# Feed-forward up projections as seven block products in place of eight, in four parts of a layer

## The chip, the cores and the metric

One Trainium2 chip, one NeuronCore. The metric is device time in microseconds (us) of one execution of the whole program, the median over runs; lower is better. Engines: PE (matrix products, with PEld for its weight loads), DVE (vector), ACT (scalar), POOL (GpSimd), SP (issues the transfers).

## What is computed

Two layers of a hybrid encoder over 512 prompt tokens and 64 sample tokens, 576 columns in all. The feed-forward is the part that the change touches; `D_MODEL` is 1024, `D_FF` is 2816:

```python
x = _layernorm(DEEPNORM_ALPHA * x + merged @ w_o, ln1_g, ln1_b)
ff = (jax.nn.silu(x @ w_ff1) * (x @ w_ff3)) @ w_ff2
x = _layernorm(DEEPNORM_ALPHA * x + ff, ln2_g, ln2_b)
```

Ahead of it every layer has one combined input projection, three attentions (forgetting, differential, sparse), three gated branch products and `w_o`. All inputs and outputs are float32.

## The kernel before

**Numbers in two pieces.** Weights and activations are split into a high piece (a rounded copy, `F32R`) and a low piece (the rest), and each product is three matmuls: high by high, high by low, low by high. A weight tile of 128x512 arrives by a transfer in a staging buffer `st` (three of them); ACT casts it to `wh` (line 331) and DVE subtracts to get `wl` (line 334). The pairs go to a ring of five slots (`RING`, line 42). The tokens lie transposed in `xT`, [128, 8, 1216]: columns 0 to 639 high, from 640 on low.

**Feed-forward.** The 22 blocks of 128 hidden units are done in two parts of 11 (`FF_SPLIT`, line 28). For each block, `s_block` (line 382) makes `x @ w_ff1` and then `x @ w_ff3`: two PSUM banks for the column halves 256 and 320, eight steps over the 1024 inputs, three matmuls and two halves a step, 48 matmuls (line 397). `ff_pair` (line 1624) follows: tanh on ACT (line 1632), two DVE operations from PSUM (lines 1633 and 1643), and the split of the 576-column result into `gT` (ACT line 1650, DVE line 1651). The first block is done by `s_first` (line 406, matmul line 418), half by half, since half 1 holds tokens that come out of the layer norm earlier. After 11 blocks `t_group` (line 356) makes the down projection, `w_ff2`: for two column halves c of 512, five token tiles by 11 blocks, three matmuls each (two for the sample tile; lines 347 to 353), the last blocks tile by tile (`tail`). `adds` (line 1658) adds each tile to `r` on DVE; in the last part c = 1 goes wholly tile by tile (`tail=nf`, line 1784), in the order 4, 3, 2, 0, 1, and each tile goes through `layernorm` (lines 514 to 543: statistics, a power on POOL, three DVE operations of 128x512, one on ACT, one addition on POOL) and, but in the last layer, through `to_xt` (transposes line 441, ACT line 446, DVE line 447) into the next layer's `xT`.

**Order.** Nothing is scheduled by the compiler. The planner `Pace` (line 96) replays the program as it is written, with a cost for each operation, a time from engine to engine (`LAG`) and priorities, and writes each engine's instructions in the order that comes out; on the chip each engine works through its list in that order, waiting for semaphores. `either` lets the planner choose between two engines, `late` makes one of them less welcome.

Of the kernel before, what the change touches and what calls it, by code (L numbers as in the profile page):

```python
# [18 lines left out]
D = 1024  # L19
# [7 lines left out]
NFB = DFF // 128  # L27
FF_SPLIT = (11, 11)
ALPHA = (2 * DEPTH) ** 0.25
# [213 lines left out]
def hybrid_step(ctx, tc, A, O):  # L243
# [56 lines left out]

    def loader(units):
        for u in units:
            st, was = yield take(stage)
            go(fetch(u, st, was))

    def fetch(u, st, was):
        n = 1
# [11 lines left out]
        came = yield dma(128 * n * 4, load, was, 1.5 if u.no == 0 else 4 if u.no < 4 else 5)  # L319
        if u.dest is None:  # L320
            u.slot, free = yield take(ring, u.no)
            hi, lo = u.slot
        else:
            free = yield wait(u.dest[0])
            hi, lo = u.dest[1]()

        def urgent():
            gap = u.no - Unit.used
            return 2 if gap <= 1 else 6 if gap == 2 else 12
# [7 lines left out]
        stage.give(st, down)  # L337
        u.hi, u.lo = view(hi), view(lo)
        u.flag.set(join(up, down))


# [43 lines left out]
    def s_block(units, nk, hi, lo, done, after={}):  # L385
# [16 lines left out]
        for s in range(2):  # L402
            go(done(s, ps[s][0], last))

    def s_first(blocks, X):
# [166 lines left out]

    def give_when(slots, item, flag, kind=None):
        slots.give(item, (yield wait(flag)), kind)

# [62 lines left out]
    def operands(E):  # L638
# [35 lines left out]
        s = yield dve(24, lambda: nc.vector.tensor_scalar(E.gbias, ps[:, :24], 0.5, None, op0=OP.mult), s, 12)  # L674
        banks.give(ps, s, "att")
        E.gbias_in.set(s)

# [770 lines left out]
    def new_env(l):  # L1448
# [4 lines left out]
        one = ("opened", "nt_read", "early_free", "cum", "b_open", "res0_open", "res1_open", "ffn_open",  # L1453
               "mt_open", "gbias_in", "ops", "th_in", "a_prepared")
        for nm in one:
# [7 lines left out]
        E.gb1_in, E.gb2_in = Flag(pace, 2), Flag(pace, 2)  # L1463
        E.ln1 = Flag(pace, 10)
        E.ya, E.yb, E.yc = Flag(pace, 5), Flag(pace, 5), Flag(pace, 5)
        E.close = None
        return E

    def layer_units(E):
# [40 lines left out]
        for part, nf in enumerate(FF_SPLIT):  # L1510
            for f in range(f0, f0 + nf):
                W.f1.append(sblk(w1, D, f * 128))
                W.f3.append(sblk(w3, D, f * 128))
            last = part == len(FF_SPLIT) - 1
            W.f2.append([tcols(w2, 0, f0 * 128, nf),
                         tcols(w2, 512, f0 * 128, nf, (lambda k: None) if not last else (
                             lambda k: None if k == nf - 1 else
                             (E.ffn_open, lambda: (E.res2[:, k, 0], E.res2[:, k, 1]))))])
            f0 += nf
        return W  # L1520


    def in_order(x):
        if isinstance(x, Unit):
# [86 lines left out]
    def open_ffn(E):  # L1611
# [7 lines left out]
        E.gT = fpool.tile([128, max(FF_SPLIT), XW], F32R, name="gT")  # L1619
        E.res2 = fpool.tile([128, FF_SPLIT[-1] - 1, 2, 512], F32R, name="res2")  # L1620
        E.ffn_open.set()
        yield from load_gb(E.gb2, A["ln2_g"][E.l], A["ln2_b"][E.l], E.gb2_in)

    def ff_pair(E, th, part, i):
        tanh = [Flag(pace), Flag(pace)]
        both = Flag(pace, 2)

        def one(h, ps, s):
            c, w = HALVES[h]
            t1, was = yield from th.get()  # L1630
            t = t1[:, c:c + w]
            u = yield act(w, lambda: nc.scalar.activation(t, ps[:, :w], AF.Tanh, scale=0.5), [s, was], 3, 90)  # L1632
            u = yield dve(w, lambda: nc.vector.scalar_tensor_tensor(t, t, 1.0, ps[:, :w], op0=OP.add, op1=OP.mult),  # L1633
                          [s, u], 3)
            banks.give(ps, u, "acc")
            tanh[h].set(u)

        def three(h, ps, s):
            c, w = HALVES[h]
            s = join(s, (yield wait(tanh[h])))  # L1640
# [32 lines left out]
    def layer(E, X, r_free):  # L1673
# [68 lines left out]


        go(open_ffn(E))
        done = [first, second]
        f = 0
        for part, nf in enumerate(FF_SPLIT):
            for i in range(nf):
                th = Later(th_slots)
                one, three = ff_pair(E, th, part, i)  # L1750
                if f == 0:
                    yield from s_first([(W.f1[f], one), (W.f3[f], three)], X)
                else:
                    yield from s_block(W.f1[f], 8, xT, xT_lo, one)
                    yield from s_block(W.f3[f], 8, xT, xT_lo, three)
                f += 1
            before, done = done, [flags5(), flags5()]
            final = part == len(FF_SPLIT) - 1
            if not final:
                for c in range(2):  # L1760
                    yield from t_group(W.f2[part][c], E.gT, adds(E, r, c, True, before[c], done[c]),
                                       ready=E.gT_in[part])
                continue
# [88 lines left out]
```

## Time and profile before

| | us |
|---|---|
| median of 3 runs | 2296.77 (2293.96 to 2298.13) |
| profiled execution, its own time | 2294.76 |
| span of its instructions | 2292.9 |
| PE busy in the span | 2243.2 (98%) |
| DVE, ACT, POOL busy | 1362.6, 979.0, 186.4 |
| granted TensorE clock, share of full | 0.997 |

The span is from the first instruction to the last; the execution's own time has 1.9 us more. "Busy" is the time in which an engine has at least one instruction under way. Matmuls overlap each other, so the duration of one (some 0.3 us) is longer than the distance from one start to the next.

### The profile page before, as it was taken

To read this page: it belongs to the slowest core of one execution; us is meant where nothing else is said; L and a number is where in the kernel's file an instruction comes from. 1 tells how busy PE (TensorE), PEld (TensorE's weight loads), DVE (VectorE), ACT (ScalarE), POOL (GpSimd) and SP (SyncE) were. 2 spreads that over 40 slices of the span, in tenths; PEclk is the share of its full clock that TensorE was granted. 3 is DMA by queue.
4 is the path that set the end of the run, shared out by engine and by line. 5 is a ranking of instruction groups with operands and counts; after the bars stand their busy time and mean duration, and the time that the engine had idled before them with its cause. 6 is when DMAs were issued, how large, how long until landed. Compare 5 with 4: busy or idle time off the path is not lost. (4 is left out here: it accounts for less than half of the span.)

```text
span 2292.9 us, 37910 instructions
## 1 busy us (share of the span) xinstructions
PE 2243.2 (98%) x14564; PEld 2011.9 (88%) x14572; DVE 1362.6 (59%) x2978; ACT 979.0 (43%) x2159; POOL 186.4 (8%) x146
## 2 busy tenths in 40 slices
PE   8999999999999999999999989999999999999998
PEld 7886798789998998999878868987899989989996
DVE  6979664675448443343789896537744474424436
ACT  4565664474333322232345656645743332222221
POOL 1001000201111000000120010002011110000001
PEclk9999999999999999999999999999999999999999
DMA  5321222242342332222332222222323422222222
GB/s 143 99 90 58 72 76 91 85 123 56 102 139 72 91 86 84 84 83 83 106 102 89 92 65 68 77 90 85 118 61 102 147 69 84 83 83 83 85 91 74
DMA packets 248829, 204.79 MB, mean 89 GB/s; under 512 B 24248, under 2 KB 196680, under 8 KB 248648
## 3 DMA queue, kind: packets, MB, share of 16 engines
q1 hardware_dynamic: 248648, 202.37, 29.9%
q8 instruction: 114, 1.87, 0.3%
q14 instruction: 67, 0.55, 0.1%
HBM read 178.26 MB, written 23.92 MB: 88 GB/s over the span
## 5 line engine op out<-in xcount | busy, mean ns | idle before, releaser
L397 PE MATMUL bank<-xT,wh 128*128 128x256 f32 x4416 | 767.5, 296 | 0.0
L397 PEld LDWEIGHTS bank<-xT,wh 128*128 128x128 f32 x4416 | 657.6, 188 | 4.2 <-issue 1.8
L334 DVE TENSOR_TENSOR wl<-st,wh 128x512 fp32r<-128x512 f32 x568 | 400.1, 708 | 409.2 <-ACT wh L331 404.7
L331 ACT CAST wh<-st 128x512 fp32r<-128x512 f32 x568 | 348.6, 620 | 619.6 <-PE bank L397 232.0
L397 PE MATMUL bank<-xT,wl 128*128 128x256 f32 (+1 forms) x2208 | 470.9, 294 | 0.0
L397 PEld LDWEIGHTS bank<-xT,wl 128*128 128x128 f32 x2208 | 368.4, 188 | 0.0
L347 PE MATMUL bank<-wh,xT 128*128 128x512 f32 x560 | 231.8, 414 | 0.0
L349 PE MATMUL bank<-wh,xT 128*128 128x512 f32 x560 | 220.7, 394 | 0.0
L348 PE MATMUL bank<-wl,xT 128*128 128x512 f32 x560 | 220.3, 393 | 0.0
L349 PEld LDWEIGHTS bank<-wh,xT 128*128 128x128 f32 x560 | 105.6, 189 | 23.7
L347 PEld LDWEIGHTS bank<-wh,xT 128*128 128x128 f32 x560 | 105.9, 189 | 19.5 <-ACT c L684 0.9
L348 PEld LDWEIGHTS bank<-wl,xT 128*128 128x128 f32 x560 | 106.1, 189 | 17.6
L347 PE MATMUL bank<-wh,gT 128*128 128x512 f32 x272 | 106.1, 390 | 0.0
L349 PE MATMUL bank<-wh,gT 128*128 128x512 f32 x272 | 105.9, 389 | 0.0
L348 PE MATMUL bank<-wl,gT 128*128 128x512 f32 x272 | 105.9, 389 | 0.0
L976 ACT ACTIVATE P<-bank,nm 128x128 f32<-128x128 f32 (+4 forms) x160 | 80.0, 503 | 59.5 <-DVE nm L985 55.0
L1633 DVE SCALAR_TENSOR_TENSOR th<-th,bank 128x256 f32<-128x256 f32 (+1 forms) x88 | 36.2, 451 | 98.6 <-ACT th L1632 98.6
L985 DVE TENSOR_REDUCE nm<-bank 128x1 f32<-128x384 f32 (+5 forms) x108 | 64.1, 603 | 46.2 <-PE bank L1187 24.2
L764 POOL TENSOR_TENSOR rb<-rb,rc 128x512 f32<-128x512 f32 (+1 forms) x32 | 44.8, 1399 | 563.6 <-DVE rb L759 549.3
L397 PE MATMUL bank<-yhl,wh 128*128 128x256 f32 (+1 forms) x512 | 89.4, 296 | 0.0
L1009 ACT COPY PT<-bank 128x512 f32<-128x512 f32 (+5 forms) x162 | 65.8, 449 | 50.4 <-PE bank L1000 48.3
L1643 DVE SCALAR_TENSOR_TENSOR th<-th,bank 128x256 f32<-128x256 f32 (+1 forms) x88 | 36.2, 451 | 83.1 <-PE bank L397 79.3
(250 smaller groups left out, 3694.1 us busy)
## 6 DMA issues: line engine op xcount, KB each, us to landing
st<-in_w_ff SPq DMA_DIRECT2D x264, 256.0 KB, 2.9
st<-in_w_in SPq DMA_DIRECT2D x256, 256.0 KB, 2.8
st<-in_w_o SPq DMA_DIRECT2D x32, 256.0 KB, 2.9
out<-c SPq DMA_DIRECT2D x18, 256.0 KB, 2.2
m_park<-th SPq DMA_DIRECT2D x16, 288.0 KB, 2.1
merged<-m_park SPq DMA_DIRECT2D x16, 288.0 KB, 5.1
out<-abt SPq DMA_DIRECT2D x16, 256.0 KB, 2.6
st<-in_w_br_a SPq DMA_DIRECT2D x16, 256.0 KB
```

The lines of the kernel that those rows point to most:

```text
L331: up = yield act(n, lambda: nc.scalar.copy(hi[:, :n], st[:, :n]), [came, free], urgent)
L334: return lambda: eng.tensor_tensor(lo[:, :n], st[:, :n], hi[:, :n].bitcast(F32), op=OP.subtract)
L347: nc.tensor.matmul(ps, lhsT=h, rhs=u.hi, start=first, stop=False)
L348: nc.tensor.matmul(ps, lhsT=h, rhs=u.lo, start=False, stop=False)
L349: nc.tensor.matmul(ps, lhsT=lo, rhs=u.hi, start=False, stop=last)
L397: nc.tensor.matmul(ps[s][0][:, :w], lhsT=x[:, kk], rhs=y[:, k, c:c + w], start=(k == 0 and i == 0), stop=(k == nk - 1 and i == 2))
L764: return lambda: eng.tensor_tensor(x[:n], x[:n], buf[:n], op=OP.add)
L976: s = yield act(nk, lambda: nc.scalar.activation(P[:n, j * nk:(j + 1) * nk], S[:n, j * nk:(j + 1) * nk], AF.Exp, bias=nm[:n, j:j + 1], sca ...
L985: return dve(hb * nk, lambda: nc.vector.tensor_reduce(st[0][:n, :hb], S[:n, :hb * nk].rearrange("p (a b) -> p a b", a=hb), axis=AX.X, op=O ...
L1009: ends.append((yield either(act(w, lambda: nc.scalar.copy(PTs[:kw, sl, :n], PT[:kw, sl, :n]), s, 8), late(dve(w, lambda: nc.vector.tensor_ ...
L1633: u = yield dve(w, lambda: nc.vector.scalar_tensor_tensor(t, t, 1.0, ps[:, :w], op0=OP.add, op1=OP.mult), [s, u], 3)
L1643: s = yield dve(w, lambda: nc.vector.scalar_tensor_tensor(t, t, 0.5, ps[:, :w], op0=OP.mult, op1=OP.mult), s, 3)
```

## The change

The weight of two neighbouring blocks of hidden units (1024 inputs by 256 units) is taken as a 2 by 2 matrix of blocks [512 x 128], and the tokens as a 2 by 2 matrix of blocks [512 inputs x 288 columns]. In place of the eight block products a `Group` makes seven, from sums of weight blocks and sums of token blocks, and joins them in PSUM: `seven` makes each as 12 matmuls of 288 columns, lets ACT copy a bank into another one where two results share a part (`start_copy`), and lets DVE add the second product from an SBUF buffer (`added`). 20 of the 22 blocks of a layer go this way (10 groups for `w_ff1`, 10 for `w_ff3`); the first two stay as they were (`PLAIN`). Four sums of weight blocks are made in a group, two on DVE and two on POOL, and seven pieces are split in place of four tiles. The sums of tokens are made once in a layer (`token_sums`). Since the sums and eight `raw` buffers need SBUF, `gT` becomes shorter: the feed-forward is done in parts of 6, 6, 6 and 4 blocks. A matmul of 288 columns opens each bank once in a layer (`seeded`).

```diff
-FF_SPLIT = (11, 11)
+FF_SPLIT = (6, 6, 6, 4)
+PLAIN = 2
+HT = NTOK // 2
+RAW = 8
+EXTRA = 2
...
+        def prepare(self):
+            E, p, came = self.E, self.pieces, self.came
+            if self.before is not None:
+                yield wait(self.before.seated)
+            a11, a21, a22 = self.raw[:3]
+            t = self.sum
...
+            def seat(i, tile, s, made):
+                u = p[i]
+                u.slots = E.more if i in (2, 5) else ring
+                u.slot, free = yield take(u.slots, u.no)
...
+            made = [Flag(pace) for _ in range(7)]
+            in11 = yield wait(came[0])
+            yield from seat(0, a11, in11, made[0])
+            in21 = yield wait(came[1])
+            in22 = yield wait(came[2])
+            s1 = yield comb(t, a21, a22, OP.add, [in21, in22, self.was_sum], "D")
+            yield from seat(1, t, s1, made[1])
+            s3 = yield comb(a21, a11, a21, OP.subtract, [in11, s1], "G")
+            d1 = yield wait(made[1])
+            s2 = yield comb(t, t, a11, OP.subtract, [s1, d1], "D")
+            yield from seat(2, t, s2, made[2])
+            in12 = yield wait(came[3])
+            a12 = self.raw[3]
+            yield from seat(3, a12, in12, made[3])
+            yield from seat(4, a21, s3, made[4])
+            d3 = yield wait(made[3])
+            s4 = yield comb(a12, a12, t, OP.subtract, [d3, s2], "G")
+            yield from seat(5, a12, s4, made[5])
+            yield from seat(6, a22, in22, made[6])
+            self.seated.set()
...
+    def seven(group, E, done):
+        x = join((yield wait(E.sums_in)), (yield wait(E.tmp_free)))
...
+            def emit():
+                for kk in range(4):
+                    for j, (w, part) in enumerate(((u.hi, 0), (u.hi, 1), (u.lo, 0))):
+                        nc.tensor.matmul(bank[:, :HT], lhsT=w[:, kk], rhs=y(kk, part), start=begin and kk == 0 and j == 0,
+                                         stop=kk == 3 and j == 2, skip_group_check=True)
+            s = yield pe(cols(HT, 12), emit, [ok, x, s])
...
+        def start_copy(to, frm, s, flag):
+            flag.set((yield act(HT, lambda: nc.scalar.copy(to[:, :HT], frm[:, :HT]), s, 2, 60)))
...
+        def added(h, bank, s, out):
+            s = join(s, (yield wait(side.flag)))
+            e = side.got
+            s = yield dve(HT, lambda: nc.vector.tensor_tensor(bank[:, :HT], bank[:, :HT], e, op=OP.add), s, 2)
+            side.read.set(s)
+            go(out(h, bank, s))
...
+        a, was = yield bank_acc()
+        p1 = yield from product(0, a, raw(0, 0), True, was)
+        b, was = yield from seeded()
+        go(start_copy(b, a, [p1, was], c[0]))
+        e, was = yield bank_acc()
+        go(aside(e, (yield from product(1, e, made(0), True, was))))
+        u = yield from product(2, b, made(1), False, (yield wait(c[0])))
+        g, was = yield from seeded()
+        go(start_copy(g, b, [u, was], c[1]))
+        c11 = yield from product(3, a, raw(4, 0), False, (yield wait(c[0])))
+        go(done[0](0, a, c11))
+        u7 = yield from product(4, b, made(2), False, (yield wait(c[1])))
+        d, was = yield from seeded()
+        go(start_copy(d, b, [u7, was], c[2]))
+        c12 = yield from product(5, g, raw(4, HT), False, (yield wait(c[1])))
+        go(added(1, g, c12, done[0]))
+        go(added(1, b, join(u7, (yield wait(c[2]))), done[1]))
+        c21 = yield from product(6, d, made(3), False, (yield wait(c[2])))
+        go(done[1](0, d, c21))
+
+    def token_sums(E, X):
+        s = yield from all_of(X.made)
+        yield wait(E.ffn_open)
...
+        for k0 in (0, 2):
...
+                at[r, c] = yield either(dve(2 * HT, whole(nc.vector), [s, used], 5),
+                                        late(gps(2 * HT, whole(nc.gpsimd), [s, used], 5), 0))
...
+            t1 = yield minus(x11, x12, x11, [at[0, 0], at[0, 1]])
+            t3 = yield minus(x12, x22, x12, [at[1, 1], t1])
+            t2 = yield minus(x22, x22, x11, [t1, t3])
+            d1 = yield from parts(0, x11, t1)
+            t4 = yield minus(x21, x21, x22, [t2, at[1, 0]])
+            d2 = yield from parts(1, x22, t2)
+            d3 = yield from parts(2, x12, t3)
+            d4 = yield from parts(3, x21, t4)
+            used = join(d1, d2, d3, d4, t4)
+        E.tmp_free.set(used)
...
         go(open_ffn(E))
+        go(token_sums(E, X))
...
+                two = [ff_pair(E, Later(th_slots), part, i + j, ((0, HT), (HT, HT))) for j in range(2)]
+                for m, g in enumerate((W.f1[f], W.f3[f])):
+                    yield from seven(g, E, [fns[m] for fns in two])
+                i, f = i + 2, f + 2
```

### What moves in the engines' lists

DVE, layer 0, from the end of the first layer norm on (`th` is the work of the first plain blocks, `xT` the last token tile's low piece). Before:

```order
L447 TENSOR_TENSOR xT<-bank_70,xT 128x4x128
L1643 SCALAR_TENSOR_TENSOR th_113<-th_113,bank_69 128x320
L1633 SCALAR_TENSOR_TENSOR th_113<-th_113,bank_74 128x256
L1643 SCALAR_TENSOR_TENSOR th_113<-th_113,bank_73 128x256
L334 TENSOR_TENSOR wl_77<-st_88,wh_76 128x512
L334 TENSOR_TENSOR wl_81<-st_87,wh_80 128x512
L1651 TENSOR_TENSOR gT<-th_113,gT 128x576
```

Now:

```order
L652 TENSOR_TENSOR xT<-bank_70,xT 128x4x128
L1866 SCALAR_TENSOR_TENSOR th_113<-th_113,bank_69 128x320
L586 TENSOR_TENSOR tmp<-xT 128x576
L586 TENSOR_TENSOR fifths<-xT 128x576
L591 TENSOR_TENSOR tmp<-tmp 128x576
L591 TENSOR_TENSOR tmp<-fifths,tmp 128x576
L591 TENSOR_TENSOR fifths<-fifths,tmp 128x576
L1856 SCALAR_TENSOR_TENSOR th_113<-th_113,bank_74 128x256
L596 TENSOR_TENSOR sums<-tmp,sums 128x576
L591 TENSOR_TENSOR tmp<-tmp,fifths 128x576
L395 TENSOR_TENSOR raw_6682<-raw_6680,raw_6681 128x512
```

From behind the `xT` row to the last write of `sums` there are 39 operations on DVE: 20 of 128x576 for the token sums (lines 586, 591, 596), two `gT`, eight weight splits, two weight sums and seven of the two plain blocks' own. POOL has four additions of line 586 and two of line 396 in the same stretch. Layer 1 has the same order.

ACT, in the middle of the blocks of a layer. Before:

```order
L331 CAST wh_82<-st_87 128x512
L331 CAST wh_84<-st_86 128x512
L1650 CAST gT<-th_113 128x576
L331 CAST wh_78<-st_88 128x512
L1632 ACTIVATE th_112<-bank_75 128x256
L1632 ACTIVATE th_112<-bank_68 128x320
```

Now (`bank<-bank` is a start copy, `fifths` a product set aside, `raw` a block or sum of weights, `gT` the end of the pair before):

```order
L352 CAST wh_78<-raw_6680 128x512
L1873 CAST gT<-th_113 128x576
L1873 CAST gT<-th_112 128x576
L532 COPY bank_71<-bank_74 128x288
L352 CAST wh_76<-raw_6679 128x512
L1796 CAST gT<-gT 128x64 x2
L536 COPY fifths<-bank_69 128x288
L352 CAST wh_80<-raw_6683 128x512
L532 COPY bank_72<-bank_71 128x288
```

Before, ACT's list in the blocks had casts, tanh and `gT` alone, and PE waited for none of them but through a weight tile or a bank; now PE's third product of a group stands behind the first copy of this piece.

DVE, the last layer norm (line 707 adds a tile of the down projection to `r`, line 747 is the last addition of a tile). Before:

```order
L542 TENSOR_TENSOR r<-r,gb_16586 128x512
L502 TENSOR_TENSOR r<-r,bank_71 128x512
L514 BN_STATS st_107<-r 128x6
L519 BN_AGGR mv_111<-st_107 128x2
L520 TENSOR_SCALAR mv_111<-mv_111 128x1
L522 SCALAR_TENSOR_TENSOR mv_111<-mv_111 128x1
```

Now:

```order
L747 TENSOR_TENSOR r<-r,gb_16745 128x512
L724 BN_AGGR mv_111<-st_107 128x2
L707 TENSOR_TENSOR r<-r,bank_72 128x512
L725 TENSOR_SCALAR mv_111<-mv_111 128x1
L707 TENSOR_TENSOR r<-r,bank_74 128x512
L719 BN_STATS st_105<-r 128x6
```

Before, a tile's chain stood behind the tile before it, undivided; now the next tiles' additions stand inside it, since a tile is four blocks of matmuls and not eleven.

## Rows read from the trace of the kernel before

**Rows 1.** Page, parts 1: the span, and busy time, share, instructions of two engines.

```profile
span 2292.9 us, 37910 instructions
...
PE 2243.2 (98%) x14564; PEld 2011.9 (88%) x14572; DVE 1362.6 (59%) x2978; ACT 979.0 (43%) x2159; POOL 186.4 (8%) x146
```

**Rows 2.** Windows: the two feed-forward stages, busy time of each engine (instructions), clock, DMA.

```profile
740.00:1109.00 369.00, 369.00 (x2473) 351.09 (x2472) 151.25 (x272) 106.36 (x194) 0.00 (x0) 1.00 0.31 90
1877.00:2245.00 368.00, 368.00 (x2474) 350.44 (x2473) 149.58 (x269) 105.72 (x192) 0.00 (x0) 1.00 0.30 89
```

**Rows 3.** Chain of waits, layer 1: start us, us, what; unbroken runs of up-projection matmuls.

```profile
1877.82 126.39 PE bank L397 x960
...
2074.06 139.04 PE bank L397 x1056
```

**Rows 4.** Groups by form on PE: busy us, mean ns of one, idle before.

```profile
L397 PE MATMUL bank<-xT,wh 128*128 128x320 f32 x2208 | 631.5, 309 | 0.0
L397 PE MATMUL bank<-xT,wh 128*128 128x256 f32 x2208 | 605.9, 283 | 0.0
```

**Rows 5.** Timeline, layer 0, first norm and first block: start us, us, engine, line.

```profile
699.32 0.68 DVE L499 SCALAR_TENSOR_TENSOR r<-r,bank 64x512 f32<-64x512 f32 x1
...
732.70 1.29 DVE L447 TENSOR_TENSOR xT<-bank,xT 128x512 fp32r<-128x512 f32 x2 [1.32 <-ACT xT L446]
...
734.05 0.38 PE L418 MATMUL bank<-xT,wh 128*128 128x256 f32 x1 [0.45 <-DVE xT L447]
...
739.50 0.68 PE L397 MATMUL bank<-xT,wh 128*128 128x256 f32 x4
```

**Rows 6.** Timeline, DVE in the first blocks: two operations back to back in one row.

```profile
740.24 1.29 DVE L334 TENSOR_TENSOR wl<-st,wh 128x512 fp32r<-128x512 f32 x2
...
746.59 0.81 DVE L1633 SCALAR_TENSOR_TENSOR th<-th,bank 128x256 f32<-128x256 f32 x2
```

**Rows 7.** Timeline, POOL and DVE at 61 us.

```profile
61.15 1.29 POOL L764 TENSOR_TENSOR rb<-rb,rc 64x512 f32<-64x512 f32 x1 [1.65 <-DVE rb L759]
...
61.39 1.61 DVE L334 TENSOR_TENSOR wl<-st,wh 128x512 fp32r<-128x512 f32 x1 [0.41 <-ACT wh L331]
```

**Rows 8.** Groups by form on DVE and POOL: busy us, mean ns, idle before.

```profile
L541 DVE TENSOR_TENSOR r<-r,gb 128x512 f32<-128x512 f32 x32 | 20.7, 688 | 0.5
...
L542 DVE TENSOR_TENSOR r<-r,gb 128x512 f32<-128x512 f32 x16 | 25.1, 1570 | 0.4
...
L764 POOL TENSOR_TENSOR rb<-rb,rc 128x512 f32<-128x512 f32 x26 | 36.3, 1396 | 537.3 <-DVE rb L759 527.0 <-ACT P L1052 5.2 <-ACT c L684 5.1
...
L543 POOL TENSOR_TENSOR r<-r,gb 128x512 f32<-128x512 f32 x16 | 26.3, 1641 | 28.3 <-DVE r L541 28.3
```

**Rows 9.** Timeline, PE, end of layer 0: its last column half begins; layer 1's half 0.

```profile
1109.73 0.39 PE L352 MATMUL bank<-res,gT 128*128 128x512 f32 x1
...
1159.93 0.38 PE L418 MATMUL bank<-xT,wh 128*128 128x256 f32 x1 [0.34 <-DVE xT L447]
```

**Rows 10.** Chain of waits, the end of the program.

```profile
2269.81 0.23 PE bank L349
...
2282.73 0.24 PE bank L349
...
2287.61 1.63 DVE r L542
```

**Rows 11.** Windows in layer 1's attentions and a wait there: columns as in rows 2.

```profile
1317.00:1323.10 6.10, 2.96 (x16) 1.99 (x16) 5.91 (x12) 4.16 (x8) 1.53 (x2) 1.00 0.22 86
1323.20:1326.50 3.30, 3.30 (x9) 2.53 (x9) 3.20 (x6) 0.79 (x2) 0.00 (x0) 0.50 0.50 159
...
1322.97 0.67 PE L352 MATMUL bank<-wh,xT 128*128 128x512 f32 x1 [1.86 <-DVE rb L735]
```

**Rows 12.** Groups by form on ACT: busy us, mean ns, idle before.

```profile
L331 ACT CAST wh<-st 128x512 fp32r<-128x512 f32 x568 | 348.6, 620 | 619.6 <-PE bank L397 232.0 <-PE bank L352 207.7 <-issue 112.1
...
L1009 ACT COPY PT<-bank 128x256 f32<-128x256 f32 x28 | 10.3, 374 | 5.3 <-PE bank L1000 4.8 <-ACT Qd L957 0.4
```

More of the change, by code (lines that the diff above doesn't have):

```diff
@@ L301, in loader, with fetch @@
     def loader(units):
+        group = None
         for u in units:
+            if isinstance(u, Group):
+                yield wait(u.E.ffn_open)
+                u.before, group = group, u
+                for j in range(4):
+                    u.raw[j], u.was[j] = yield take(u.E.raws)
+                    go(u.load(j))
+                    if j == 2:
+                        u.sum, u.was_sum = yield take(u.E.raws)
+                        go(u.prepare())
+                continue
             st, was = yield take(stage)
-            go(fetch(u, st, was))
-    def fetch(u, st, was):
+            go(fetch(u, st, was, group))
+    def fetch(u, st, was, group):
         n = 1
@@ L320, in fetch @@
         if u.dest is None:
+            if group is not None:
+                yield wait(group.seated)
             u.slot, free = yield take(ring, u.no)
@@ L325, in fetch, with split @@
             hi, lo = u.dest[1]()
+        yield from split(u, st, n, hi, lo, came, free, view)
+        stage.give(st, u.split)
+    def split(u, st, n, hi, lo, came, free, view):
         def urgent():
@@ L403, in s_block, with raw, made, product @@
             go(done(s, ps[s][0], last))
+    def seven(group, E, done):
+        x = join((yield wait(E.sums_in)), (yield wait(E.tmp_free)))
+        def raw(k0, c):
+            return lambda kk, part: xT[:, k0 + kk, part * LX + c:part * LX + c + HT]
+        def made(i):
+            return lambda kk, part: E.sums[:, i, part, kk]
+        def product(i, bank, y, begin, s):
+            u = group.pieces[i]
+            ok = yield wait(u.flag)
+            if begin:
+                E.whole.add(id(bank))
+            def emit():
[4 more added lines that the diff above has]
+            s = yield pe(cols(HT, 12), emit, [ok, x, s])
+            u.free(s)
+            return s
+        def seeded():
+            bank, s = yield bank_acc()
+            if id(bank) not in E.whole:
+                E.whole.add(id(bank))
+                s = yield pe(cols(HT), lambda: nc.tensor.matmul(bank[:, :HT], lhsT=xT[:, 0, :128], rhs=xT[:, 0, :HT],
+                                                                start=True, stop=True), [s, x])
+            return bank, s
+        def start_copy(to, frm, s, flag):
+            flag.set((yield act(HT, lambda: nc.scalar.copy(to[:, :HT], frm[:, :HT]), s, 2, 60)))
+        def aside(e, s):
+            buf, was = yield take(E.fifth, 3)
+            s = yield act(HT, lambda: nc.scalar.copy(buf, e[:, :HT]), [s, was, x], 3, 60)
+            banks.give(e, s, "acc")
+            side.got = buf
+            side.flag.set(s)
+            E.fifth.give(buf, (yield wait(side.read)))
+        def added(h, bank, s, out):
[4 more added lines that the diff above has]
+            go(out(h, bank, s))
+        side = Env()
+        side.flag, side.read = Flag(pace), Flag(pace, 2)
+        c = [Flag(pace) for _ in range(3)]
+        a, was = yield bank_acc()
[17 more added lines that the diff above has]
+        go(done[1](0, d, c21))
@@ L571, in get, with give_when @@
             return self.item, was
[L573 to L574 removed]
+    def give_when(slots, item, flag, kind=None, more=()):
+        slots.give(item, join((yield wait(flag)), *more), kind)
     def all_of(flags):
@@ L1760, in layer @@
                 for c in range(2):
-                    yield from t_group(W.f2[part][c], E.gT, adds(E, r, c, True, before[c], done[c]),
+                    yield from t_group(W.f2[part][c], E.gT, adds(E, r, c, part == 0, before[c], done[c]),
                                        ready=E.gT_in[part])
```

110 lines of the change are left out of this document (91 added, 19 removed).

## Prediction

> **What bounds the kernel now.** I read the busy times first: PE is busy for 2243.2 of 2292.9 us, DVE for 59% and ACT for 43% [rows 1]. That share alone does not say that a matmul less is time less, so I went to the windows of the two feed-forward stages. There PE is busy for 369.00 of 369 and 368.00 of 368 us, with DVE at 150 to 151 (41%), ACT at 106 (29%), POOL at nothing, and the clock at full [rows 2]. The chain of waits says the same in another way: 960 and 1056 up-projection matmuls follow each other without one wait [rows 3]. So the stage that the change works on is purely PE's, and what is taken from PE there counts in full, as long as nothing else takes its place. The reader should look at what has room: DVE has 218 us free in 369, but not everywhere. Around the two layer norms it is DVE that sets the pace: the first norm's five tiles take DVE from 699.32 to 733.99 us, some 7 us a tile, with hardly a pause [rows 5].
>
> **The matmuls (−62.2 us).** 3840 matmuls of 256 and 320 columns go, 3360 of 288 columns and eight opening ones come: 472 fewer. The distance from one start to the next is 126.39 us / 960 = 0.1317 us in a mix of equal numbers of 256 and 320 [rows 3]; 288 is the middle of the two, and the durations of the two forms, 283 and 309 ns, differ by about what 64 columns cost [rows 4], so I take 0.1317 for 288 as well. 472 x 0.1317 = 62.2 us. The Trainium skill, on its page "TensorE: Matmul & The Clock Gate", section Back-to-back issue gap, gives N/2.4 + 2.5 ns for a lone stream; at 288 columns that would be 122.5 ns, and the saving 57.8 us in place of 62.2. The row is slower than the rule by 9 ns a matmul, and the row decides. The down projection keeps its matmuls.
>
> **The start of each feed-forward (+26 us, 11 to 33).** All seven products wait for the token sums, the first one too, though it reads none. The sums can begin when the last piece of `xT` is written, at 733.99 in layer 0 [rows 5]. From there DVE's list has 39 operations to the last sum: 22 of 576 columns, ten of 512, seven of 256 to 320. Back to back a 512-wide one takes 1.29 − 0.69 = 0.60 us [rows 6], a 576-wide one by the same rate 0.675, a pair of the small ones 0.81 [rows 6]. That is 14.9 + 6.0 + 2.8 = 23.7 us. In the same stretch POOL adds six times, and there a price comes in that the change does not show: a subtraction on DVE that began 0.24 us after a POOL addition took 1.61 us in place of 0.69, 0.92 more, and ended 0.56 us after POOL did [rows 7]; additions that always run beside POOL's average 1570 ns, the same form without it 688 [rows 8]. Both read two SBUF operands, as all the sums do. POOL's 512-wide addition takes 1.40 us alone [rows 8], a 576-wide one by that rate 1.57. Four of these, on which the differences wait, cost DVE 6.3 us and the two narrower ones 0.92 each: 8.1. So the sums stand at 23.7 + 8.1 = 31.8 us after `xT`. PE's own work until then is half 0, 739.50 − 734.05 = 5.45 us [rows 5], and 96 matmuls of the second block, 12.6: 18.1 us. PE then waits 13.7; I take 13 a layer, since a POOL addition may lie partly beside an operation that reads PSUM. Below, without any blocking, it is 23.7 − 18.1 = 5.6; above, with POOL at 1.64 us as in its other group [rows 8], 16.3.
>
> **The end of each feed-forward (+20 us, 14 to 23).** In the last column half the tiles now end after 4 blocks and not 11, so seven blocks, 7 x 14 x 0.23 [rows 10] = 22.5 us of PE's work, no longer stand beside the norms. Layer 0: before, 50.2 us pass from the first matmul of that half to layer 1's half 0, which needs all of `xT` [rows 9]; less 22.5 that leaves 27.7. Now DVE sets it: first tile 8 x 0.23 = 1.8, 0.2 to DVE, and the 34.7 us that the same five tiles take it in the first norm [rows 5]: 36.7, so +9. Layer 1: without `xT` (5.6 us) and 0.9 of other work in that stretch it is 28.2, so DVE ends 30.2 after the half began. Before it ended 35.4 (154 matmuls) + 6.3 after it (2287.61 + 1.63 − 2282.97) [rows 10], and 41.7 − 22.5 = 19.2: +11. The tiles' chains now lie inside each other, which can hide up to 3 us of waiting for POOL in each: hence 14.
>
> **The clock (+3.4 us, 0 to 7).** After waits of 1.9 us and one before it, the granted clock stood at 0.50, 1.2 GHz, for 3.30 us, and then at 1.00 again [rows 11]. PE has no wait of that length in the feed-forward now; ahead of the first group it would stand for some 10 us. I count one such stretch a layer, 3.3 / 2 = 1.7 us of work lost.
>
> **Inside the groups (+4 us, 0 to 32).** For two blocks PE now has 14 x 12 x 0.1317 = 22.1 us. DVE has 18 operations of 512, 12 of 288 and two of 576: 10.8 + 4.8 + 1.4 = 17.0 us, and four POOL additions that cost it up to 0.92 each: 20.7, or 94%. ACT has 14 casts, ten copies and the tanh and `gT` casts, 31 operations of at most 0.62 [rows 12], below 16 us. Weight pieces have a lead of seven products, 11 us, so their lateness is covered. What is not covered is ACT's list: a start copy has one product, 1.58 us, from the end of the bank that it reads to the product that needs it; itself it takes about 0.40 (0.374 at 256 columns), and a cast that has just begun ahead of it 0.62 [rows 12]. With 0.2 for each way, 0.2 to 0.8 is left. Ahead of it ACT may wait for a sum or a `gT` that DVE makes, so a block of 0.92 on DVE can reach PE with some 0.4. I let one in eight of the 80 additions do so: 4 us. All of them: 32.
>
> The added additions to `r` (40 more on DVE), the seven splits for four, and the transfers (the same megabytes) I cost at nothing: the down projections cover them. From the last pair of a part to the end of the next part's first pair DVE's list has 46 operations of 512 (weight splits, additions to `r`, sums of weights), 12 of 288 and two `gT`, 27.6 + 4.8 + 1.4 = 33.8 us, beside some 60 us of PE (22.1 for the pair, 6 x 28 x 0.23 = 38.6 for the down projection). If that cover went, the groups' DVE share would be over 100%, and the third rival below would be the result.
>
> **The sum.** −62.2 + 26 + 20 + 3.4 + 4 = −8.8 us against the profiled execution's 2294.76: 2286.0. The median of the runs lies 2.0 above that execution, so 2288.0 beside 2296.77. A difference under 0.2%, 4.6 us, is what a measurement of this kernel can hardly tell from none.
>
> **The rivals.**
> - *The starts are hidden* (0.15). DVE and POOL do not stand in each other's way here, and the planner's order gets the sums done 5.6 us late; no stalls in the groups, no clock lost: −62.2 + 11 + 20 = −31, 2266. For it: DVE is only 41% busy [rows 2]. Against it: [rows 7, 8].
> - *Starts and ends at their upper ends* (0.10): 33 + 23 in place of 26 + 20 gives 2298, no difference that can be told.
> - *The groups go at the pace of DVE and ACT* (0.22). POOL's additions make DVE late, ACT waits in its list, and the start copies behind it come too late for PE. At 0.4 us each, the gain of 12.8 that is left without this term is gone from 32 of the 80 additions on; with 65 of them it is 26 us, 2310, slower than before. For it: each mid-part pair asks 94% of DVE, in a fixed order that knows nothing of the blocking. Against it: the lead of seven products, and a down projection after at most three pairs.
>
> **How the numbers follow.** The forecast, the terms as I took them, has 0.53: 2288, and from 2280 to 2299 by the bounds of the two large terms, of which 0.38 lies under 2292 and 0.15 between 2292 and 2301. With the first rival that makes faster 0.53, with the second one same 0.25, and the third is slower, 0.22. The range of eight in ten goes from the first rival to a little past the third: 2264 to 2314; the forecast's own is 2280 to 2299.
>
> **What would show it.** In the new profile: matmuls of 288 columns 0.13 us apart; a wait of some 13 us on PE ahead of the first product of each layer's groups, released by DVE's last subtraction of the sums; DVE operations with two SBUF operands at 1.5 us beside POOL's; PE done some 17 us before the end, not 6; in the groups short waits on ACT's copies that sum up to a few us. I am wrong if PE's wait ahead of the groups is under 6 us, or if the groups themselves take over 23 us a pair.

## The result and the profile after

| | before | after |
|---|---|---|
| median, us | 2296.77 | 2269.69 (2268.16 to 2271.98, 5 runs) |
| ratio to before | | 0.9884, 95% interval 0.9869 to 0.9898 |
| span of the profiled execution | 2292.9 | 2267.4 |
| PE busy | 2243.2 | 2196.1 |
| DVE, ACT, POOL busy | 1362.6, 979.0, 186.4 | 1617.9, 1116.4, 319.7 |

The changed kernel is 27.1 us (1.2%) faster. The forecast was 8.8 us, with a range of 2264 to 2314; the time lies in the range and on the side that was forecast, but outside the forecast's own 2280 to 2299, and nearer the first rival's 2266 than the forecast's 2288.

**Where the time went.** Four marks divide the two executions: the first matmul of column half 0 of the feed-forward's first block in layer 0, the first matmul of half 0 of layer 1's first products, the same as the first mark in layer 1, and the end. The timeline on PE, the marks in the kernel before:

```profile
733.21 0.38 PE L418 MATMUL bank<-xT,wh 128*128 128x256 f32 x1 [0.28 <-ACT xT L446]
1159.20 0.39 PE L418 MATMUL bank<-xT,wh 128*128 128x256 f32 x1 [0.24 <-ACT xT L446]
1871.38 0.38 PE L418 MATMUL bank<-xT,wh 128*128 128x256 f32 x1 [0.28 <-ACT xT L446]
```

and in the changed kernel:

```profile
734.02 0.38 PE L623 MATMUL bank<-xT,wh 128*128 128x256 f32 x1 [0.28 <-ACT xT L651]
1148.45 0.40 PE L623 MATMUL bank<-xT,wh 128*128 128x256 f32 x2
1858.37 0.39 PE L623 MATMUL bank<-xT,wh 128*128 128x256 f32 x1 [0.28 <-ACT xT L651]
```

Layer 0's feed-forward goes from 425.99 to 414.43 us (−11.6), layer 1's, to the end of the span, from 421.5 to 409.0 (−12.5). The stages that the change does not touch differ by +0.8 up to the first mark and −2.3 in layer 1's attentions. In the kernels below these stages differ by as much without an edit there (layer 1's take 708.6 to 713.5 us), so I count it as scatter.

So each feed-forward gains 12 us. The matmuls alone are worth 28.5 us a layer (below); some 16 go back, at two places.

**The groups themselves.** The chain of waits (start us, us, what) has a part of three pairs as one unbroken row, in both layers:

```profile
844.47 67.11 PE bank L516 x504
...
1968.22 67.10 PE bank L516 x504
```

That is 67.11 / 504 = 0.1332 us for a matmul of 288 columns, and not one wait. The windows of this part, its down projection and two further stretches (columns as in [rows 2]):

```profile
762.00:766.60 4.60, 4.60 (x19) 4.60 (x20) 4.52 (x6) 1.15 (x3) 1.66 (x1) 0.50 0.58 168
844.50:911.50 67.00, 67.00 (x505) 66.90 (x504) 59.30 (x94) 39.50 (x88) 15.94 (x11) 1.00 0.31 91
911.70:949.70 38.00, 38.00 (x170) 31.45 (x169) 18.62 (x28) 9.45 (x17) 1.29 (x1) 1.00 0.30 89
1130.00:1146.00 16.00, 11.31 (x56) 10.54 (x57) 15.18 (x27) 5.07 (x9) 8.88 (x10) 0.68 0.31 110
```

In the groups PE is busy for all of 67.00 us, with DVE at 59.30 of 67 (89%); in the down projection DVE falls to half. In layer 0's feed-forward the granted clock is below full in two places: behind the wait at the first group (0.50, that is 1.2 GHz, at 762 us) and in the norm at the end of layer 0 (0.68, where the kernel before has 1.00 from 1109 to 1160 us).

**The first group.** Timeline on PE, layer 0:

```profile
753.13 0.43 PE L516 MATMUL bank<-xT,wh 128*128 128x288 f32 x2
...
755.65 0.29 PE L516 MATMUL bank<-sums,wh 128*128 128x288 f32 x1
757.08 0.40 PE L516 MATMUL bank<-sums,wh 128*128 128x288 f32 x1 [1.14 <-DVE sums L596]
...
757.72 0.29 PE L516 MATMUL bank<-sums,wl 128*128 128x288 f32 x1
761.88 0.61 PE L516 MATMUL bank<-sums,mh 128*128 128x288 f32 x1 [3.86 <-ACT bank L532]
```

The first product starts at 753.13, right behind the plain blocks, while DVE still works on the token sums. The second one stops 1.3 us for the second half of its sum, the third one 4.0 us for a start copy of ACT: 5.3 us of waiting. Up to there DVE has no room (windows, columns as in [rows 2]):

```profile
734.00:753.00 19.00, 18.53 (x144) 18.34 (x145) 18.93 (x26) 8.25 (x16) 6.47 (x4) 1.00 0.49 149
753.00:762.00 9.00, 4.00 (x29) 3.53 (x27) 9.00 (x16) 5.97 (x12) 1.74 (x1) 0.91 0.11 29
```

It is busy for 18.93 of 19.00 and 9.00 of 9.00 us. The third product's first matmuls then go at half rate. In the chain 36 matmuls and an opener take from 761.88 to 769.41, 7.5 us in place of 4.9:

```profile
761.88 3.25 PE bank L516 x12
...
765.36 4.05 PE bank L516 x24
769.55 4.78 PE bank L516 x36
```

Layer 1 waits 5.5 us there and loses 2.0 to the clock.

**POOL beside DVE.** Timeline on DVE in the same stretch: four operations of 0.68 to 0.75 us that take longer beside POOL's additions; and the end of the last sum.

```profile
735.11 1.21 DVE L586 TENSOR_TENSOR tmp<-xT 128x576 f32<-128x576 f32 x1
...
741.75 1.74 DVE L355 TENSOR_TENSOR wl<-st,wh 128x512 fp32r<-128x512 f32 x1
...
746.62 2.00 DVE L596 TENSOR_TENSOR sums<-tmp,sums 128x576 fp32r<-128x576 f32 x1
748.55 1.93 DVE L355 TENSOR_TENSOR wl<-raw,wh 128x512 fp32r<-128x512 f32 x1
...
761.92 0.75 DVE L596 TENSOR_TENSOR sums<-tmp,sums 128x576 fp32r<-128x576 f32 x1
```

With one more of 1.12 us these are 4.4 us of being held up. The groups by form show the same for the whole kernel (busy us, mean ns, idle before): a split beside POOL's weight sums takes 957 ns on average, one elsewhere 719.

```profile
L355 DVE TENSOR_TENSOR wl<-st,wh 128x512 fp32r<-128x512 f32 x422 | 301.1, 719 | 232.6 <-ACT wh L352 228.6 <-PE bank L1178 0.9 <-PE bank L1562 0.7
L355 DVE TENSOR_TENSOR wl<-raw,wh 128x512 fp32r<-128x512 f32 x200 | 189.9, 957 | 17.9 <-ACT wh L352 15.8
```

**The end.** Timeline of PE's last matmul, in the kernel before and in the changed one, and of DVE's last addition in the changed one:

```profile
2282.57 0.39 PE L349 MATMUL bank<-wh,gT 128*128 128x512 f32 x1
```

```profile
2248.49 0.39 PE L440 MATMUL bank<-wh,gT 128*128 128x512 f32 x1
```

```profile
2262.09 1.63 DVE L747 TENSOR_TENSOR r<-r,gb 128x512 f32<-128x512 f32 x1
```

PE's last matmul begins 18.9 us before the end of the span, 10.4 before the change (2282.57 of 2292.92); the chain of that time is almost all DVE's. In layer 0 the last 12 us before the second mark are PE's again: from 1136.57 to 1148.45 us it has no wait, and the chain has 20 matmuls of layer 1's half 1 at half clock,

```profile
1137.32 5.58 PE bank L623 x20
```

0.28 us each in place of 0.147 (the half's later ones, 9 in 1.32 us).

### The profile page after: what moved, and what is told of

The parts are those of the page before. It is cut to its first block, busy times and chain, and to the rows that moved or that the text cites. A ratio compares the mean times of both kernels' runs of the same rounds, so it can differ in the third digit from the quotient of the medians.

```text
span 2267.4 us, 37802 instructions
## 1 busy us (share of the span) xinstructions
PE 2196.1 (97%) x14092; PEld 1964.5 (87%) x14100; DVE 1617.9 (71%) x3308; ACT 1116.4 (49%) x2501; POOL 319.7 (14%) x234
## 4 chain that ended last, share of the span: by engine, by line
PE 81%; DVE 12%; issue 4%; POOL 1%; ACT 1%; DMA 1%; SPq 0%; POOLq 0%; DVEq 0%; ACTq 0%
PE bank L488 20%; PE bank L516 20%; PE bank L438 8%; PE bank L440 8%; PE bank L439 8%; PE bank L1177 2%; PE bank L1367 2%; PE bank L1206 2%; PE bank L443 2%; PE bank L444 2%; PE bank L623 2%; PE bank L1178 2%; DVE wl L355 2%; DVE rc L962 1%; PE bank L1528 1%
## 5 line engine op out<-in xcount | busy, mean ns | idle before, releaser
L488 PE MATMUL bank<-xT,wh 128*128 128x256 f32 x1856 | 326.4, 298 | 0.0
L488 PEld LDWEIGHTS bank<-xT,wh 128*128 128x128 f32 x1856 | 275.6, 188 | 4.1 <-issue 1.8
L355 DVE TENSOR_TENSOR wl<-raw,wh 128x512 fp32r<-128x512 f32 x200 | 189.9, 957 | 17.9 <-ACT wh L352 15.8
L516 PE MATMUL bank<-sums,wh 128*128 128x288 f32 x960 | 195.6, 295 | 2.5 <-DVE sums L596 2.5
L488 PE MATMUL bank<-xT,wl 128*128 128x256 f32 (+1 forms) x928 | 197.9, 295 | 0.0
L352 ACT CAST wh<-raw 128x512 fp32r<-128x512 f32 x200 | 123.1, 619 | 77.0 <-PE bank L443 62.5
L516 PEld LDWEIGHTS bank<-sums,wh 128*128 128x128 f32 x960 | 154.0, 188 | 2.9 <-DVE sums L596 2.9
L488 PEld LDWEIGHTS bank<-xT,wl 128*128 128x128 f32 x928 | 154.9, 188 | 0.0
L516 PE MATMUL bank<-sums,wl 128*128 128x288 f32 x480 | 141.5, 295 | 0.0
L516 PE MATMUL bank<-xT,wh 128*128 128x288 f32 x640 | 131.4, 297 | 0.0
L438 PEld LDWEIGHTS bank<-wh,xT 128*128 128x128 f32 x560 | 106.2, 190 | 19.6 <-ACT c L890 0.9
```

The costliest lines, as they stand in the source:

```text
L352: up = yield act(n, lambda: nc.scalar.copy(hi[:, :n], st[:, :n]), [came, free], urgent)
L438: nc.tensor.matmul(ps, lhsT=h, rhs=u.hi, start=first, stop=False)
L488: nc.tensor.matmul(ps[s][0][:, :w], lhsT=x[:, kk], rhs=y[:, k, c:c + w], start=(k == 0 and i == 0), stop=(k == nk - 1 and i == 2))
L516: nc.tensor.matmul(bank[:, :HT], lhsT=w[:, kk], rhs=y(kk, part), start=begin and kk == 0 and j == 0, stop=kk == 3 and j == 2, skip_group_c ...
```

## Experiments

Ten kernels. All times are medians beside runs of the kernel before on the same chip (2295.99 to 2296.74 us). The changed kernel ran only in the first set; differences to it compare medians of different sets, in which the kernel before lay within 0.8 us of itself. The four marks divide each profiled execution, so that the feed-forwards can be told from the stages that no edit touches. After the result the theory was: the gain of the matmuls is real and full; what is given back lies at the first group of each layer (token sums not ready) and at the end of each layer (last part too short); the groups cost nothing.

**1. The four parts alone**, in the kernel before:

```diff
-FF_SPLIT = (11, 11)
+FF_SPLIT = (6, 6, 6, 4)
```

This kernel multiplies `r` by the norm's factor in each of the three first parts and not in one, so it computes something else than the layer; the operations are as many as in the changed kernel's parts, and either form of them takes some 0.68 us.

> The kernel before with one line changed: the feed-forward in parts of 6, 6, 6 and 4 blocks, no block products. Theory (the end of a layer costs because its last column half has tiles of 4 blocks and not 11, so that the norms stand alone): the matmuls stay, layer 0 loses 9 us at its end and layer 1 8.5, with some 1 us of half clock behind the wait: 2296.8 + 18.5 = 2315 us, and PE done some 19 us before the program ends. Rival (the ends are long because DVE and POOL are crowded by sums of the groups): 2297 us, PE done 10 us before the end.

Measured: 2316.3 us, ratio 1.008 (1.0058 to 1.0102): 19.6 us slower, for 18.5 expected. The feed-forwards take 434.8 and 430.3 us, 8.8 more each; the rest lies in the stages without an edit. Timeline: PE's last matmul begins at 2295.42, the span ends at 2314.4, 19.0 us later.

```profile
2295.42 0.39 PE L349 MATMUL bank<-wh,gT 128*128 128x512 f32 x1
```

The end term belongs to the split into parts and has nothing to do with the block products.

**2. Four plain blocks ahead of the groups**

```diff
-PLAIN = 2
+PLAIN = 4
```

> The changed kernel with four plain blocks ahead of the groups and not two. Theory (PE's wait at the first group, 5.6 us a layer, and the half clock behind it, 2.2, are the token sums not being ready): both go, 15.6 us in two layers; two blocks by eight products in place of seven cost 192 x 0.1317 - 168 x 0.1332 = 2.9 us a layer: 2269.7 - 15.6 + 5.8 = 2260 us. Rival (the wait is one of a first group as such: its copies on ACT, its weights): it stays and moves by two blocks, 2269.7 + 5.8 = 2275 us.

Measured: 2261.98 us (ratio 0.9848, 0.9830 to 0.9865), 7.7 faster than the changed kernel, for 9.7 expected; the feed-forwards alone are 5.2 and 4.5 us shorter, which is the 9.7. In the chain PE goes from the plain blocks into the first groups without a stop, and the first product of a group takes 1.59 us, at full rate:

```profile
741.08 37.92 PE bank L488 x288
779.00 1.59 PE bank L516 x12
```

So the wait is not one of a first group as such. It is that for the token sums and what stands between them in DVE's list; 25 us more of other work on PE hide it, at the price of one pair of blocks without the saving.

**3. Parts of 4, 6, 6 and 6**

```diff
-FF_SPLIT = (6, 6, 6, 4)
+FF_SPLIT = (4, 6, 6, 6)
...
-                             lambda k: None if k == nf - 1 else (E.more_free, lambda: E.taken[k]) if k < EXTRA else
+                             lambda k: None if k > EXTRA else (E.more_free, lambda: E.taken[k]) if k < EXTRA else
...
-        E.res2 = fpool.tile([128, FF_SPLIT[-1] - 1 - EXTRA, 2, 512], F32R, name="res2")
+        E.res2 = fpool.tile([128, 1, 2, 512], F32R, name="res2")
```

> The changed kernel with parts of 4, 6, 6 and 6 blocks; in the last column half three weight tiles wait in the ring of five and not one, as there is no room for more resident ones. Theory (tiles of 4 blocks are too short to cover the norms): two blocks more stand beside them, 2 x 14 x 0.23 = 6.4 us a layer, as long as DVE is behind: 2269.7 - 12.8 = 2257 us, PE done 12.5 us before the end and not 18.9. Rival (DVE's order of the chains is what takes the time, whatever PE does beside it; or the ring with three slots taken holds up the next layer's first weights): 2270 us or more.

Measured: 2261.67 us (0.9846, 0.9829 to 0.9863), 8.0 faster than the changed kernel. The feed-forwards take 409.3 and 404.7 us, 5.2 and 4.3 less, for 6.4 expected; the last matmul begins 14.1 us before the end and not 18.9. Theory, at two thirds to four fifths of its price: what is missing was not separated (DVE's chains of the norms, or the three ring slots that are taken).

**4. The token sums on DVE alone**

```diff
-                at[r, c] = yield either(dve(2 * HT, whole(nc.vector), [s, used], 5),
-                                        late(gps(2 * HT, whole(nc.gpsimd), [s, used], 5), 0))
+                at[r, c] = yield dve(2 * HT, whole(nc.vector), [s, used], 5)
```

> The changed kernel with all first additions of the token sums on DVE, none on POOL. Theory (POOL's additions hold DVE up for about as long as DVE would take for them itself): DVE has 4 x 0.67 = 2.7 us more a layer and loses some 3 us of being held up (operations of 1.21, 2.00 and 1.93 us in place of 0.75, 0.75 and 0.68): within 2 us of 2269.7. Rival (POOL's help is real and the wait at the first group ends with DVE's list): 2 x 2.7 = 5.4 us more, 2275 us.

Measured: 2277.11 us (0.9911, 0.9893 to 0.9928): slower by 7.4, near the rival's time. Of the 8.5 us by which the profiled execution is longer, 1.5 and 2.5 lie in the feed-forwards; 0.9 and 3.6 lie in the stages before them, which the edit does not touch. And what the feed-forwards lose is not lost for the rival's reason. From half 0's first matmul (734.90) to the start of the last token sum (761.37) 26.5 us pass, in the changed kernel 27.9 (734.02 to 761.92): DVE is done earlier without POOL's help. But PE waits 6.75 us for the start copy. The timeline of POOL, ACT and PE says why:

```profile
759.04 4.80 POOL L396 TENSOR_TENSOR raw<-raw,raw 128x512 f32<-128x512 f32 x1 [9.31 <-ACT sums L594]
763.87 0.62 ACT L352 CAST mh<-raw 128x512 fp32r<-128x512 f32 x1 [3.87 <-POOL raw L396]
764.40 0.61 ACT L352 CAST wh<-raw 128x512 fp32r<-128x512 f32 x1
764.92 0.39 ACT L532 COPY bank<-bank 128x288 f32<-128x288 f32 x1
765.36 0.61 PE L516 MATMUL bank<-sums,mh 128*128 128x288 f32 x1 [6.75 <-ACT bank L532]
```

A weight sum on POOL took 4.80 us, where 1.30 is the median of its kind in the changed kernel; a cast of ACT waited 3.87 us for it, and the start copy stands behind that cast in ACT's list. DVE ran operations with two SBUF operands without a pause from 758.23 until 762.72, and POOL's addition ended 1.1 us after that:

```profile
758.83 0.74 DVE L595 TENSOR_TENSOR sums<-fifths,sums 128x576 fp32r<-128x576 f32 x1
...
762.04 0.68 DVE L355 TENSOR_TENSOR wl<-raw,wh 128x512 fp32r<-128x512 f32 x1
764.52 0.69 DVE L355 TENSOR_TENSOR ml<-raw,mh 128x512 fp32r<-128x512 f32 x1 [1.80 <-ACT mh L352]
```

The Trainium skill, on its page "SBUF — State Buffer", section "Who interferes with whom", says that of the two engines the one that issues second is fully blocked, whichever it is. The trace agrees that it goes both ways, 2.00 us for a DVE operation of 0.75 and 4.80 for a POOL addition of 1.30; the POOL addition here stood through six DVE operations, not one.

**5. Each product waits, in the plan, for its own token sum**

```diff
-        x = join((yield wait(E.sums_in)), (yield wait(E.tmp_free)))
...
+            x = (yield wait(E.sums_in[{1: 0, 2: 1, 4: 2, 6: 3}[i]])) if i in (1, 2, 4, 6) else {}
...
```

> The changed kernel, planned with each product waiting only for the token sum that it reads, so that the first start copy stands five rows earlier in ACT's list (ahead of three casts of token sums). Theory (the wait at the first group is DVE's list of work: sums, splits and weight sums): the low piece of the third product's weights and the last part of its token sum keep their places in that list within two rows, so PE's wait ends within 1 us of where it did: 2268 to 2271 us. Rival (PE waits only because the copy stands behind casts in ACT's list): the third product starts 2.4 us earlier in each layer, 2265 us.

Measured: 2270.87 us (0.9883, 0.9869 to 0.9898), no difference. PE's waits in layer 0 become 1.5, 1.9 and 1.6 us, 5.0 in all for 5.3. The third product starts 25.7 us after the first mark and not 27.9, nearly as much earlier as the rival said, but it stops again at 763.57, for 1.13 us, until DVE has written its `sums`. The copy's place in ACT's list alone was not the limit: DVE's list is as long as before.

**6. All weight sums on DVE**

```diff
-            s3 = yield comb(a21, a11, a21, OP.subtract, [in11, s1], "G")
+            s3 = yield comb(a21, a11, a21, OP.subtract, [in11, s1], "D")
...
-            s4 = yield comb(a12, a12, t, OP.subtract, [d3, s2], "G")
+            s4 = yield comb(a12, a12, t, OP.subtract, [d3, s2], "D")
```

> The changed kernel with all four sums of weight blocks of a group on DVE and none on POOL. Theory (the groups have room, and POOL's additions cost DVE about what they take off it): 80 more additions of 0.60 us, 48 us, and the splits beside POOL's additions fall from a mean of 957 ns to about 720, 200 x 0.24 = 48 us: DVE's busy time within 15 us of 1618, no wait of PE in the groups, 2267 to 2273 us. Rival (DVE is close to its limit in the groups): waits of PE in the groups, 2280 us or more.

Measured: 2269.65 us (0.9882, 0.9866 to 0.9899), no difference. DVE has 80 instructions more and is busy for 1602.8 us, 15.1 less than in the changed kernel. Groups by form on DVE:

```profile
L355 DVE TENSOR_TENSOR wl<-raw,wh 128x512 fp32r<-128x512 f32 x200 | 135.7, 684 | 16.8 <-ACT wh L352 16.4
L395 DVE TENSOR_TENSOR raw<-raw,raw 128x512 f32<-128x512 f32 x160 | 109.6, 685 | 8.4 <-DMA raw<-in_w_ff 6.8
```

The splits fall from 957 to 684 ns. POOL's additions took 54.2 us from DVE in these splits alone (189.9 − 135.7), and 6.8 in those of `ml`; the 80 additions more on DVE are 54.6. A POOL addition saves DVE nothing here.

**7. Both: POOL adds nothing at the first group** (the edits of 4 and 6)

> Both moves at once: token sums and weight sums all on DVE, so POOL adds nothing at the first group. Theory from the run with the token sums alone on DVE (PE's wait of 6.9 us ended late because a cast of weights, ahead of the start copy in ACT's list, waited for a POOL addition that took 4.80 us beside a busy DVE): that addition now takes 0.7 us on DVE and the wait is some 2 us shorter in each layer, 2277 - 4.5 = 2272 us. Rival (DVE's list alone sets it): two more operations in it, 2278 us or more.

Measured: 2273.17 us (0.9890, 0.9876 to 0.9905), 3.9 faster than run 4, for 4.5 expected; the feed-forwards are 2.1 and 2.7 us shorter than there. The waits in layer 0 are 1.7, 1.7 and 1.4 us, 4.8 in all, and the row on the start copy is now

```profile
767.06 0.85 PE L516 MATMUL bank<-sums,mh 128*128 128x288 f32 x2 [1.12 <-ACT bank L532]
```

That agrees with the cause found in run 4. The wait is close to the changed kernel's 5.3 with any sharing of the sums but that of run 4: what bounds it is DVE's list. The 3.5 us to the changed kernel do not lie in the feed-forwards, which take 413.9 and 408.8 us for 414.4 and 409.0; the first mark comes 5.9 us later in this execution (739.87 for 734.02), in a stage without an edit.

**8. Four plain blocks and parts of 4, 6, 6 and 6** (the edits of 2 and 3)

> The changed kernel with four plain blocks and parts of 4, 6, 6 and 6. Theory (the wait at the start and the short last part are two costs that do not touch each other): the gains of the two single runs add up, 2269.7 - 7.7 - 8.0 = 2254 us. Rival (one of them hides the other, or the first part without groups moves the wait elsewhere): 2258 us or more.

Measured: 2254.4 us, ratio 0.9815 (0.9800 to 0.9830): 15.3 us faster than the changed kernel and 42 faster than the kernel before, the best version here. The two costs are independent: 7.7 + 8.0 = 15.7, and in the feed-forwards 10.4 and 9.1 us are gained where runs 2 and 3 together gain 10.3 and 8.9.

**9 and 10. How far the groups are from DVE's pace.** Useless additions on DVE in the chain of each group's weight sums, four, then eight:

```diff
+            if self.before is not None and self.before.E is E and self.before.before is not None and self.before.before.E is E:
+                d1 = join(d1, (yield wait(E.tmp_free)), (yield wait(E.gb2_in)))
+                for _ in range(4):
+                    d1 = yield dve(512, lambda: nc.vector.tensor_tensor(E.tmp[:, 0, :512], E.gb2[:, 0, :512], E.gb2[:, 1, :512], op=OP.add), [s1, d1], 5)
```

> The changed kernel with four useless DVE additions of 128x512 (two SBUF operands, into a scratch buffer) in the chain of each group's weight sums, from a layer's third group on: 4.8 us more DVE work a pair of blocks, where DVE is now busy for 59.3 of 67.0 us in three pairs. Theory (the lead of seven products, 11 us, covers a DVE that falls behind by less than that, and the down projection lets it catch up): 14.4 - 7.7 = 6.7 us behind after three pairs, no wait of PE in the groups, 2268 to 2274 us. Rival (the groups go at DVE's pace as soon as it has more work than PE): 6.7 us in each of four parts of three pairs and 4.4 in each of four of two, 2269.7 + 44 = 2314 us.

> The same with eight useless additions a group, 9.6 us a pair. Theory: 28.8 - 7.7 = 21 us behind after three pairs, of which the lead covers 11: PE waits some 10 us in each of the four long parts and 3 in each short one, 2269.7 + 52 = 2322 us, with waits released by splits of weights on DVE late in each part. Rival (all of it shows): 21 and 14 us a part, 2410 us; or none of it, 2270, if DVE's list lets the needed splits pass ahead of the sums.

Measured: 2301.56 us with four (ratio 1.0022, 1.0013 to 1.0032), 2417.97 with eight (1.0526, 1.0509 to 1.0544). The theory falls in both. A part of three pairs with four (window of its groups):

```profile
844.50:917.80 73.30, 69.01 (x507) 67.36 (x506) 68.60 (x114) 39.29 (x87) 21.22 (x11) 1.00 0.28 83
```

and with eight:

```profile
851.60:943.10 91.50, 74.51 (x505) 71.66 (x504) 87.33 (x137) 41.66 (x89) 18.86 (x11) 0.94 0.23 67
```

The part takes 73.3 and 91.5 us for 67.1: 6.2 and 24.4 more, where the expectations put the overload at 6.7 and 21 (by their 0.60 us an addition DVE would have 110% and 132% of PE's 67.0 us to do). About the whole overload shows, with eight somewhat more, in part at a lower clock (0.94); a lead of seven products covers none of it. DVE is busy for 94% and 95% of these windows, so even here not all the time. The additions stand one behind the other in the chain of a group's weight sums, and what they cost as a chain was not separated from what they cost as work. The waits on PE in the whole program (us in total, times, longest), in the changed kernel,

```profile
PE bank L516 <- ACT bank L532: 7.7, 2, 3.9
```

with four,

```profile
PE bank L520 <- ACT bank L536: 22.1, 14, 3.9
```

and with eight:

```profile
PE bank L520 <- ACT mh L352: 53.4, 30, 2.8
PE bank L520 <- DVE ml L355: 45.7, 36, 1.7
```

(Lines 532 and 536 are the start copy, 516 and 520 the product.) The 7.7 us are the first groups. With four additions PE waits for late start copies, with eight for the weight pieces themselves, as was expected, but for much longer. The short parts lose less than the rival's 4.4 (1.2 and 2.2 in layer 0), hence 32 us and not 44 with four.

## Why the prediction came out as it did

The terms, as forecast and as measured on the two profiled executions (span 25.5 us shorter, where 8.8 were forecast):

| term | forecast | measured |
|---|---|---|
| matmuls | −62.2 | −57.1 |
| start of each feed-forward | +26 | +10.8 (5.3 and 5.5) |
| half clock behind it | +3.4 | +4.6 (2.6 and 2.0) |
| end of each feed-forward | +20 | +17.6 (9.1 and 8.5) |
| inside the groups | +4 | 0 |
| other stages | 0 | −1.5 |
| sum | −8.8 | −25.6 |

The end's 9.1 is what is left of layer 0's −11.6 after 28.5 for the matmuls, 5.3 and 2.6; layer 1's 8.5 is the longer tail, 18.9 − 10.4, seen directly. In layer 0 it can be seen directly too: from the first matmul of the last column half to the mark 36.2 us pass (1112.30 to 1148.45), before 49.5 (1109.73 to 1159.20), less 22.5 for the seven blocks: 9.2.

**Matmuls: right, 5 us too much.** "I take 0.1317 for 288 as well": 288 columns cost 0.1332, 1.5 ns more than the middle of 256 and 320, and 3360 x 0.0015 = 5.0. The formula on the Trainium skill's page "TensorE: Matmul & The Clock Gate", section Back-to-back issue gap, led to a saving of 57.8, near the measured 57.1 but by accident: its 122.5 ns for 288 is 11 ns under the row.

**The start: the step that failed.** "All seven products wait for the token sums, the first one too, though it reads none." On the chip the first product waits for nothing, the second for its own sum, the third for a start copy: the wait on all sums is one of the planner's replay, which settles the order of the lists, and the chip's waits follow what an instruction reads. The start missed by 15.2 of the 16.8 us that lie between the forecast's sum and the measured one. About half of that is the misread wait, 4.1 us a layer, and about half the price of the blocking, 3.9. The 13.7 us a layer go, but for 0.3, into four pieces: the sums' list takes 27.9 us for 31.8 (3.9 less; POOL's additions held DVE up by 4.4 and not by 8.1, as one addition had run before the list began and another lay at its very start); two products with 3.3 us run ahead of the last stop; the third goes on 0.8 before the last sum is done; 5.3 to 5.5 are left. That DVE's list sets the place is right (runs 2, 5, 7), and so is the blocking (runs 4, 6). The text said "I am wrong if PE's wait ahead of the groups is under 6 us", and it is.

**The clock: right at the start**, a stretch at 0.50 in each layer as in [rows 11], 1.2 us more in all than counted. The stretch in the norm at the end of layer 0 (0.68 from 1130 to 1146 us) stood in no term; what it costs lies inside the end's 9.1.

**The end: right**, +9 and +11 forecast, 9.1 and 8.5 measured, and run 1 shows 8.8 us in each feed-forward for this term alone, in the kernel before. In layer 0 the match is in part luck: the forecast has DVE's pace alone set the time to the mark (36.7 us, measured 36.2), but its last 12 us were PE's, half of them at half clock.

**The groups: nothing of the +4 came.** DVE was put at 94% there; it is at 89% [window 844.50], and no blocked operation reached a product. The forecast let one block in eight through. What the runs show is a threshold somewhere above: with DVE busy for 86% (run 6, 57.4 of 67.0 us) and 89% nothing shows, with loads put at 110% and 132% about all of the overload (runs 9, 10); nothing was measured between.

**The rivals.** The first one gave nearly the right time (2266) with a wrong reason: DVE and POOL do stand in each other's way. The third (the groups at DVE's and ACT's pace, 0.22) did not come, but its mechanism is real, late start copies and all, and only 7.7 us of DVE in 67 away.

## What to carry to other kernels

A wait that a planner or scheduler models is not yet a wait of the chip: ask for each instruction what it reads itself, and cost the first instruction that really stops. Where one engine paces and another follows at some 90%, cost what is added to the follower at nothing while room is left and in full beyond it, as here at 89% and at some 110%, and see how much room the fullest stretch has, not the mean. Work that hides under matmuls in the middle of a stage has to be looked at again at its two ends, where there is less to hide it under; here both were mended by parameters (four plain blocks, the short part first), for 15 us more.

## What the runs showed of the hardware

- A POOL addition with two SBUF operands beside DVE operations of the same kind costs DVE on average at least what the addition takes on DVE itself (957 ns a split for 684; 61.0 us in the splits for 54.6, run 6), and can itself stand through six DVE operations in a row (4.80 us for 1.30, run 4).
- Matmuls of 288 columns follow each other at 133.2 ns, those of 256 and 320 in equal numbers at 131.7 [rows 3].
- Behind two stops of 1.3 and 4.0 us the granted clock was 0.50 for 4.6 us; without the stops (run 2) a product's 12 matmuls took 1.59 us in place of 3.25.
